# Feed-forward activations of both token halves turned in one go, the first input turned raw, and other orders at three places

## The chip, the cores and the metric

One core of a Trainium2 chip runs the whole program. The metric is the device time of one execution in microseconds (us); lower is better. Five engines work side by side, each through its own queue of instructions in a fixed order: PE (matrix products and transpositions), DVE (vector work), ACT (scalar activations and copies), POOL, and SP, which here does little but issue DMA transfers. An instruction waits at the head of its queue until what it needs is there, and all that stands behind it in that queue waits too.

## The reference, cut to what matters

The input is 256 tokens of 1024 features. Two layers follow, each a half feed-forward, a mixer, and another half feed-forward; the mixer is attention with pooling in layer 0 and a state-space layer (S5) with a gated output (GLU) in layer 1.

```
def _rmsnorm(x, g):
    xf = x.astype(jnp.float32)
    y = xf * lax.rsqrt(jnp.mean(xf * xf, axis=-1, keepdims=True) + EPS)
    return (y * g.astype(jnp.float32)).astype(x.dtype)

def _swiglu(h, w_gate, w_up, w_down):
    return (jax.nn.silu(h @ w_gate) * (h @ w_up)) @ w_down
...
    for layer in range(DEPTH):
        x = x + 0.5 * _swiglu(_rmsnorm(x, ffn_norm[layer, 0]), ffn_w_gate[layer, 0],
                              ffn_w_up[layer, 0], ffn_w_down[layer, 0])
        h = _rmsnorm(x, mix_norm[layer])
...
        x = x + mixed.astype(x.dtype)
        x = x + 0.5 * _swiglu(_rmsnorm(x, ffn_norm[layer, 1]), ffn_w_gate[layer, 1],
                              ffn_w_up[layer, 1], ffn_w_down[layer, 1])
```

The hidden width is 2816. So there are four feed-forwards, f = 0 to 3, with the attention mixer between f=0 and f=1 and the S5 mixer between f=2 and f=3.

## The kernel before, in words

**Products.** Each fp32 product is made of three matmuls on split operands (high times high, low times high, high times low). A weight arrives raw by DMA (tile `raw`, four buffers, issued on SP); ACT writes its high part `wh`, DVE the rest `wl`. Activations are split likewise: `hTh`/`hTl` is the normed input, transposed; `hh`/`hl` is the hidden activation, transposed. PE needs the contracted dimension on partitions, so both are transposed on PE (`tr`, a product with the identity, tile `sk` or `wk` in PSUM) before ACT and DVE split them.

**A feed-forward.** Tokens come in two tiles of 128, t = 0 and 1. The hidden width is done in 11 groups g of 256 columns. `GU(f, g, t, kh)` is the gate and up product of one tile for half kh of the 1024 features. Then ACT applies the activation (`sg`, L434), DVE makes the product (`pr`, L148), `hid_T` turns `pr` (two transpositions of 128x128) and has it split into `hh` and `hl`, and `dn(f, g, t)` is the down product, 12 matmuls of 512 columns into `acc`. `ffn_joint` runs the groups: 48 gate and up matmuls, `dn` of the group before for t=0, `hid_T` for t=0, `dn` for t=1, `hid_T` for t=1. `tail` ends a feed-forward: the last two `dn`s, the new x, the norm, and its transposition for what follows.

**Order.** Instructions are placed at build time by a scheduler. `prio(CHAIN)` lifts an instruction; `behind(names)` pins it behind instructions that `keep(name, ...)` has recorded; `hold` stops new weight splits until `release(names)`, which lets them go on behind the named instructions. S5 has a hand-written list of steps, `ORDER`: for each quarter k of the channels, `f` multiplies the input by the norm factor, `u` turns it, `w` is a product into the state space (32 small matmuls, copied out as `Sb` by ACT), `s` turns `Sb` back on PE and scans it on DVE, `d` and `o` are the direct and the output product, `h` makes the input of the GLU. An `x` with a number is so many warming matmuls, whose result nobody uses. `s5_put` copies the new x by 16 small DMAs on SP into the layout that S5 wants (tile `V`). While f=1 runs, `s5_build` prepares S5's matrices on DVE in its free time (tiles `E`, `X`, `b_q`, `b_st`).

**Start.** `first` loads the norm weights as one row, spreads it over all partitions by two products (`acc<-h,h`), multiplies x by it on DVE (`gained`), transposes the result and splits it; the squares for the norm factor are summed by ACT (`acc<-x`), and the factor `rstd` is applied later, in `sg` and `pr`.

Of the kernel before, what the change touches and what calls it, by code (L numbers as in the profile page):

```python
# [25 lines left out]
RING = 4  # L26
RAW = 4
CHAIN = 400
WARM = 20
WARM0 = 4  # L30
PACE = 0.8


# [8 lines left out]


ORDER = """
    f1 u1 hold s0 f2 u2 w1 s1 f3 u3 w2 s2 d0 o0 w3 s3 d1 d2 o1 x2 s4 h0 o2 d3 o3
"""
INV_FREQ = [
    1.0, 0.1939227432012558, 0.03760603070259094, 0.007292664609849453,
# [62 lines left out]
def trunk_kernel(ctx: ExitStack, tc: tile.TileContext, I, out):  # L111
# [16 lines left out]
    def sk(shape=(128, 512)):  # L128
        return work.tile(list(shape), F32, tag="sk", name="sk")
# [5 lines left out]
    def prio(n):  # L135
        return tc.high_priority(offset=n)

    def tt(o, a, b, op):
        return DVE.tensor_tensor(out=o, in0=a, in1=b, op=op)  # L139
# [19 lines left out]
    def tr(o, i, e):  # L159
        return PE.transpose(o, i, e)  # L160
# [8 lines left out]
    def keep(name, *ins):  # L169
        pins[name] = ins  # L170

    @contextmanager
    def behind(*names):

        with ExitStack() as st:
            for n in names:
                for i in pins.get(n, ()):
                    st.enter_context(tc.issue_after(i.ins))
            yield

    def hi_of(o, i):
        return ACT.activation(out=o, in_=i, func=AF.Copy)  # L182
# [77 lines left out]
    def emit_split(i):  # L260
        if units[i][0] == "K":
            n = units[i][1]
            tl = [wsp.tile([128, 2048], F32, tag=tg, name=f"K{n}") for tg in ("wh", "wl")]
            for q in range(2):
                c0 = 4096 * n + 2048 * q
                with behind("put"):
                    SP.dma_start(out=tl[q], in_=s5["dK"][:, c0:c0 + 2048])
            held[units[i]] = tl
            return
        if units[i][0] == "W":  # L270
            fill(2 * i)
            held[units[i]] = [raws.pop(2 * i + q).rearrange("p (a r j q n) -> p r j q a n", a=2, r=2, j=4, q=2)
                              for q in range(2)]
            return
        shape, places = pieces(units[i])
        h = wsp.tile([128, *shape], F32R, tag="wh", name="wh")
        l = wsp.tile([128, *shape], F32R, tag="wl", name="wl")
        for p in range(2):
            fill(2 * i + p)
            r = raws.pop(2 * i + p)  # L280
            s = places[p][1]
            with behind(*(["split"] if i + p else ["norm"])):
                for k in (slice(0, 2), slice(2, 4)) if i + p == 0 else (slice(None),):
                    hk, lk, rk = h[s][:, k], l[s][:, k], r[:, k]
                    keep("splits", hi_of(hk, rk), tt(lk, rk, hk.bitcast(F32), ALU.subtract))
                if i + p == 0:
                    pins["first"] = pins["splits"]
        held[units[i]] = (h, l)
# [26 lines left out]
    def acc_of(t):  # L315
        if t not in accs:
            accs[t] = [accp.tile([128, 512], F32, tag=f"acc{t}{c}", name=f"acc{t}{c}") for c in range(2)]
        return accs[t]
# [116 lines left out]
            stt(pr, ps[:, 1], rstds[f, t], sg, ALU.mult, ALU.mult)  # L435
        prods[f, g, t] = pr

    def hid_T(f, g, t):
        pr = prods.pop((f, g, t))
        o = slice(t * 128, (t + 1) * 128)  # L440
        if (f, g) not in hid:
            hid[f, g] = (hidp.tile([128, 2, 256], F32R, tag="hh", name="hh"),
                         hidp.tile([128, 2, 256], F32R, tag="hl", name="hl"))
        h, l = (x[:, :, o] for x in hid[f, g])
        ps = sk((128, 2, 128))
        with prio(CHAIN), behind("down" if g else "gu"):
            for m in range(2):
                tr(ps[:, m], pr[:, m * 128:(m + 1) * 128], ident)
            hi_of(h, ps)
            tt(l, ps, h.bitcast(F32), ALU.subtract)  # L450

    def down(f, g, t, c):
        w = held["d", f, g]
# [580 lines left out]
    def s5_put(t, c):  # L1034

        V = s5["V"]
        jobs = [(0, j) for j in (2 * c, 2 * c + 1)] + [(1, j) for j in range(4 * c)]
        for h, j in jobs:
            r = slice(64 * t + 16 * j, 64 * t + 16 * j + 16)
            c0 = 256 * j + 128 * h  # L1040
            with prio(CHAIN), behind("put", "rawW"):
                keep("put", SP.dma_start(out=V[r, h].rearrange("p t q g c -> p t (q g c)"), in_=xs[t][:, c0:c0 + 128]))

    def s5_scale(t, after):

# [182 lines left out]
    def glu(n, t, odd, terms, ks):  # L1228

        o = slice(t * 128, (t + 1) * 128)  # L1230
        if (n, t) not in glus:
            glus[n, t] = (sk if n % 2 else wk)((128, 2, 256))
        ps = glus[n, t]
        w = held["y", n, odd]
        for m in terms:
            x, y = (hTh, hTh, hTl)[m], w[m == 1]
            for k in ks:
                i = mm(ps, x[:, 2 * k + odd, o], y[:, k], odd == 0 and m == 0 and k == 0, odd == 1 and m == 2 and k == 3)
                if m == 2 and k == 1:
                    keep("glu", i)  # L1240
        if not (odd and terms[-1] == 2 and ks[-1] == 3):
            return
        th = tmp.tile([128, 256], F32, tag="t256", name="th")
        xv = xs[t][:, n * 256:(n + 1) * 256]
        with prio(CHAIN):
            ACT.activation(out=th, in_=ps[:, 1], func=AF.Tanh, scale=0.5)
            stt(th, th, 1.0, ps[:, 0], ALU.add, ALU.mult)
            stt(xv, th, 0.5, xv, ALU.mult, ALU.add)
        if n % 2:
            square(t, n // 2)  # L1250
# [6 lines left out]
    def S(fn, *uids):  # L1257
        steps.append((fn, uids))
# [22 lines left out]
    def dn(f, g, t, cs=(0, 1)):  # L1281
        for c in cs:
            if g < NG - 2:
                paced.add(len(steps))
            S(lambda c=c: down(f, g, t, c), ("d", f, g))

    def HID(f, g, t):
        S(lambda: hid_T(f, g, t))

    def ffn_joint(f, g0, g1):  # L1290

        for g in range(g0, g1):
            paced.add(len(steps))
            for kh in range(2):
                for t in range(2):
                    GU(f, g, t, kh)
                    if g == 1 and kh == 0:
                        HID(f, 0, t)
            if g < NG - 1:
                for t in range(2):  # L1300
                    dn(f, g - 1, t)
                    HID(f, g, t)

    def tail(f, fin_a, fin_b, each=lambda t, c: None):
        S(strict(f == 1))
        dn(f, NG - 2, 0, (0,))
        HID(f, NG - 1, 0)
        dn(f, NG - 2, 0, (1,))
        HID(f, NG - 1, 1)
        dn(f, NG - 1, 0, (0,))  # L1310
        S(lambda: x_update(0, 0.5, (0,)))
        each(0, 0)
        dn(f, NG - 1, 0, (1,))
        S(lambda: x_update(0, 0.5, (1,)))
        each(0, 1)
        fin_a()
        if f == 2:
            S(hold)
        dn(f, NG - 2, 1)
        if f == 1:  # L1320
            S(hold)
        dn(f, NG - 1, 1, (0,))
        S(lambda: x_update(1, 0.5, (0,)))
        each(1, 0)
        fin_b()
        dn(f, NG - 1, 1, (1,))
        S(lambda: x_update(1, 0.5, (1,)))
        each(1, 1)
# [27 lines left out]


    def first():
        row, one = hn[1][0:1], hn[0][0:1, 0:128]
        ACT.dma_start(out=row, in_=I["ffn_norm"][0, 0:1])  # L1360
        ACT.dma_start(out=ident, in_=cst[:, C_ID:C_ID + 128])
        for c in range(2):
            SP.dma_start(out=xs[0][:, c * 512:(c + 1) * 512], in_=I["x"][0, 0:128, c * 512:(c + 1) * 512])
        w = tmp.tile([128, 128], mybir.dt.bfloat16, tag="warm", name="warm")
        POOL.memset(w, 0.0)
        POOL.memset(one, 1.0)
        warm(WARM0, w)

        gvecs["f0"] = acc_of(1)
        for c in range(2):  # L1370
            mm(acc_of(1)[c], one, row[:, c * 512:(c + 1) * 512], True, True)
        fill(2 - RAW)
        for c in range(2):
            SP.dma_start(out=xs[1][:, c * 512:(c + 1) * 512], in_=I["x"][0, 128:256, c * 512:(c + 1) * 512])
        for c in range(2):
            square(0, c, acc_of(0)[c])
        gained(0, "f0")
        scaled(0, 0)
        warm(2, w)
        h_transpose(0)  # L1380
        pins["split"] = pins["hT"]
        ring.append(units[0])
        emit_split(0)
        state["split"] = 1
        with behind("first", "hT"):
            gained(1, "f0")

    def second():
        h_transpose(1, sk, "up")
        with behind("hT"):  # L1390
            for c in range(2):
                square(1, c, acc_of(0)[c])
        scaled(1, 0)
        accs.clear()
    S(first)

# [197 lines left out]
```

## Time and profile before

| what | value |
|---|---|
| median of three runs | 948.49 us (947.25 to 948.86) |
| the profiled execution | 948.75 us |
| its span in the trace | 947.0 us |
| PE busy | 927.9 us (98%) |
| DVE busy | 649.3 us (69%) |
| ACT busy | 445.9 us (47%) |
| mean granted clock of PE | 0.995 |

The time of an execution is some 1.75 us longer than the span of its trace. Busy shares are means over the whole span; in single stretches other engines decide. A granted clock of 1.00 is 2.4 GHz, 0.50 is 1.2 GHz.

### The profile page before, as it was taken

Reading aid. Unit: us, or ns where it says so; the run is one execution under the profiler, and the core shown is the slowest. Engines: PE = TensorE matmul, PEld = TensorE weight load, DVE = VectorE, ACT = ScalarE, POOL = GpSimd, SP = SyncE. Lnnn points to the kernel's source line nnn. Section 1 sums busy time; section 2 is a strip of 40 time slices with the busy share of each in tenths; the row PEclk is TensorE's granted clock in tenths of the full one; section 3 lists DMA queues with packets and bytes.
Section 4 is the critical chain, followed back from the end, with each engine's and each line's share of the span. In section 5 each row is a group of like instructions: output and inputs, shape, how many; then the busy total and the mean of one; then the engine's idle time right before and its main releaser. Section 6 shows DMA issues by size and latency. Waiting matters only on the chain.

```text
span 947.0 us, 13237 instructions
## 1 busy us (share of the span) xinstructions
PE 927.9 (98%) x5002; PEld 762.2 (80%) x5002; DVE 649.3 (69%) x1103; ACT 445.9 (47%) x653; POOL 60.2 (6%) x106
## 2 busy tenths in 40 slices
PE   9999999999999999999999999999879999999998
PEld 5888888889988888888788888888558788888886
DVE  5656754588867659999886557998487565554552
ACT  6544444455636444444454434445435464444440
POOL 0000000013020000000132001600000000000000
PEclk9999999999999999999999999999989999999999
DMA  7867666655476976566868655966855557556641
GB/s 242 274 194 210 197 185 197 192 159 159 134 202 200 200 201 204 156 190 183 281 200 288 186 178 160 259 184 213 292 187 177 179 174 225 178 183 198 195 136 44
DMA packets 149937, 184.59 MB, mean 195 GB/s; under 512 B 23153, under 2 KB 132657, under 8 KB 149106
## 3 DMA queue, kind: packets, MB, share of 16 engines
q1 hardware_dynamic: 146480, 175.29, 59.9%
q0 software_dynamic: 3248, 8.39, 3.5%
q8 instruction: 39, 0.64, 0.3%
q14 instruction: 24, 0.20, 0.1%
q10 hardware_dynamic: 146, 0.07, 0.0%
HBM read 173.24 MB, written 9.44 MB: 193 GB/s over the span
## 4 chain that ended last, share of the span: by engine, by line
PE 81%; DVE 12%; issue 2%; ACT 2%; DMA 1%; POOL 1%; SPq 0%; DVEq 0%; ACTq 0%; POOLq 0%
PE wk L101 47%; PE acc L101 26%; PE sk L101 7%; DVE wl L139 4%; DVE X L139 2%; DVE b_q L139 1%; POOL r L618 1%; DMA raw<-in_ffn_w_up_dram 1%; DVE b_t L139 1%; DVE hl L139 0%; DMA raw<-in_ffn_w_down_dram 0%; DVE qk L139 0%; ACT wh L182 0%; DVE pr L148 0%; ACT h L1082 0%
## 5 line engine op out<-in xcount | busy, mean ns | idle before, releaser
L139 DVE TENSOR_TENSOR wl<-raw,wh 128x1024 fp32r<-128x1024 f32 (+1 forms) x305 | 364.6, 1217 | 171.0 <-ACT wh L182 169.9
L182 ACT ACTIVATE wh<-raw 128x1024 fp32r<-128x1024 f32 (+1 forms) x305 | 312.7, 1052 | 254.6 <-PE wk L101 105.6
L101 PE MATMUL wk<-wh,hTh 128*128 128x512 f32 (+1 forms) x836 | 222.2, 385 | 1.2 <-DVE hTl L139 0.8
L101 PE MATMUL wk<-wl,hTh 128*128 128x512 f32 (+1 forms) x836 | 216.1, 377 | 0.1
L101 PE MATMUL wk<-wh,hTl 128*128 128x512 f32 (+1 forms) x836 | 215.1, 377 | 0.0
L101 PEld LDWEIGHTS wk<-wl,hTh 128*128 128x128 f32 x836 | 152.2, 189 | 30.0 <-DVE wl L139 0.5
L101 PEld LDWEIGHTS wk<-wh,hTl 128*128 128x128 f32 x836 | 151.8, 188 | 29.5
L101 PEld LDWEIGHTS wk<-wh,hTh 128*128 128x128 f32 x836 | 148.1, 189 | 28.2 <-DVE hTl L139 1.3
L101 PE MATMUL acc<-wh,hh 128*128 128x512 f32 x352 | 142.3, 404 | 1.3 <-ACT hh L182 1.3
L101 PE MATMUL acc<-wh,hl 128*128 128x512 f32 x352 | 138.8, 395 | 0.6 <-DVE hl L139 0.6
L101 PE MATMUL acc<-wl,hh 128*128 128x512 f32 x352 | 137.8, 392 | 0.0
L434 ACT ACTIVATE sg<-wk,rstd 128x256 f32<-128x256 f32 x88 | 41.6, 475 | 108.4 <-PE wk L101 103.9
L101 PEld LDWEIGHTS acc<-wh,hl 128*128 128x128 f32 x352 | 66.4, 189 | 16.3 <-DVE hl L139 1.7
L148 DVE SCALAR_TENSOR_TENSOR pr<-wk,rstd,sg 128x256 f32<-128x256 f32 x88 | 42.0, 479 | 53.0 <-ACT sg L434 52.9
L101 PEld LDWEIGHTS acc<-wh,hh 128*128 128x128 f32 x352 | 66.5, 189 | 14.1 <-ACT hh L182 1.5
L101 PEld LDWEIGHTS acc<-wl,hh 128*128 128x128 f32 x352 | 66.6, 189 | 12.8
L182 ACT ACTIVATE hh<-sk 128x256 fp32r<-128x256 f32 x88 | 32.7, 373 | 19.8 <-PE sk L101 19.7
L139 DVE TENSOR_TENSOR hl<-sk,hh 128x256 fp32r<-128x256 f32 x88 | 36.5, 418 | 3.7 <-ACT hh L182 3.7
L101 PE MATMUL sk<-ident,pr 128*128 128x128 f32 x176 | 33.6, 272 | 0.0
L101 PEld LDWEIGHTS sk<-ident,pr 128*128 128x128 f32 x176 | 24.1, 138 | 11.6 <-ACT b_br L930 0.3
L339 ACT ACTIVATE acc<-x 128x512 f32<-128x512 f32 x24 | 14.4, 600 | 25.9 <-DVE x L148 20.4
L139 DVE TENSOR_TENSOR hTl<-sk,hTh 128x512 fp32r<-128x512 f32 x24 | 17.4, 757 | 9.9 <-ACT hTh L182 9.9
(290 smaller groups left out, 627.0 us busy)
## 6 DMA issues: line engine op xcount, KB each, us to landing
raw<-in_ffn_w_up_dram SPq DMA_DIRECT2D x88, 512.0 KB
raw<-in_ffn_w_down_dram SPq DMA_DIRECT2D x88, 512.0 KB
raw<-in_ffn_w_gate_dram SPq DMA_DIRECT2D x87, 512.0 KB
raw<-in_ev_w_in_dram SPq DMA_DIRECT2D x16, 512.0 KB
raw<-in_s_w_glu_dram SPq DMA_DIRECT2D x16, 512.0 KB
raw<-in_ev_w_out_dram SPq DMA_DIRECT2D x8, 512.0 KB
K<-dK SPq DMA_DIRECT2D x4, 1024.0 KB
dK<-E POOLq DMA_DIRECT2D x36, 64.0 KB, 4.9
```

The lines of the kernel that those rows point to most:

```text
L101: i = f(*a, **k)
L139: return DVE.tensor_tensor(out=o, in0=a, in1=b, op=op)
L148: return DVE.scalar_tensor_tensor(out=o, in0=a, scalar=s, in1=b, op0=op0, op1=op1)
L182: return ACT.activation(out=o, in_=i, func=AF.Copy)
L339: keep("square", ACT.activation(out=into or acc_of(t)[c], in_=xs[t][:, s], func=AF.Square, scale=1.0 / 32.0, accum_out=sums[t][:, c:c + 1]))
L434: ACT.activation(out=sg, in_=ps[:, 0], func=AF.Silu, scale=rstds[f, t])
L618: POOL.tensor_tensor(out=r8, in0=s8, in1=mhalf.to_broadcast([128, 8]), op=ALU.pow)
```

## The change

There are five parts.

A. `hid_T` takes both token tiles: for groups 1 to 9 of each feed-forward the four transpositions stand in a row between the two `dn`s, ACT writes one `hh` of 128x512 and DVE one `hl` of 128x512, in place of two of 128x256 each. These are 36 places. The first and last groups keep the old form.

B. At the end of f=1, `hold` comes before the second half of the last group and `release("hid")` after the two `hid_T`, so the weight splits for f=2 go behind the `hh` and `hl`.

C. At the start the norm weights are loaded as 8x128 and turned by one transposition into a column form (`gT`); x is transposed as it is, and the split applies `gT` as a per-partition factor, one ACT copy and one DVE operation for each of 16 blocks of 128x128. The two spreading products, the four DVE products and two warming matmuls go; the four squares move behind the splits.

D. In S5 the puts have another order, so that the first half of every row group is issued by the ninth put on SP, and one put goes to ACT's queue; in `ORDER` the steps `w1 s1` and `w2 s2` stand ahead of `u2` and `u3`, with four and three warming matmuls beside them; 16 instead of 20 warming matmuls stand ahead of S5.

E. In the GLU the pin for the transposition of the next feed-forward's input (8 transpositions, `wk<-ident,h`) is moved from the last matmuls of the GLU to ten matmuls earlier.

```diff
-WARM = 20
-WARM0 = 4
+WARM = 16
+WARM0 = 5
...
-    f1 u1 hold s0 f2 u2 w1 s1 f3 u3 w2 s2 d0 o0 w3 s3 d1 d2 o1 x2 s4 h0 o2 d3 o3
+    f1 u1 hold s0 w1 s1 x4 f2 u2 w2 s2 x3 f3 u3 d0 o0 w3 s3 d1 d2 o1 x2 s4 h0 o2 d3 o3
...
-    def hid_T(f, g, t):
-        pr = prods.pop((f, g, t))
-        o = slice(t * 128, (t + 1) * 128)
+    def hid_T(f, g, *ts):
...
+        o = slice(ts[0] * 128, (ts[-1] + 1) * 128)
         h, l = (x[:, :, o] for x in hid[f, g])
-        ps = sk((128, 2, 128))
+        ps = sk((128, 2, len(ts) * 128))
         with prio(CHAIN), behind("down" if g else "gu"):
-            for m in range(2):
-                tr(ps[:, m], pr[:, m * 128:(m + 1) * 128], ident)
-            hi_of(h, ps)
-            tt(l, ps, h.bitcast(F32), ALU.subtract)
+            for n, t in enumerate(ts):
+                pr = prods.pop((f, g, t))
+                for m in range(2):
+                    tr(ps[:, m, n * 128:(n + 1) * 128], pr[:, m * 128:(m + 1) * 128], ident)
+            keep("hid", hi_of(h, ps), tt(l, ps, h.bitcast(F32), ALU.subtract))
...
-        jobs = [(0, j) for j in (2 * c, 2 * c + 1)] + [(1, j) for j in range(4 * c)]
-        for h, j in jobs:
+        if t == 0:
+            jobs = [(0, h, j) for h in range(c + 1) for j in range(2 * c * (1 - h), 2 * c * (1 - h) + 2)]
+        else:
+            jobs = [(1, 0, j) for j in (2 * c, 2 * c + 1)]
+            if c:
+                jobs += [(0, 1, 2), (0, 1, 3)] + [(1, 1, j) for j in range(4)]
+        for t, h, j in jobs:
...
-                if m == 2 and k == 1:
+                if odd == 0 and m == 2:
                     keep("glu", i)
...
+                if f == 1 and g == NG - 1 and kh:
+                    S(hold)
...
-                for t in range(2):
-                    dn(f, g - 1, t)
-                    HID(f, g, t)
+                dn(f, g - 1, 0)
+                HID(f, g, 0, 1)
+                dn(f, g - 1, 1)
...
         HID(f, NG - 1, 1)
+        if f == 1:
+            S(lambda: release("hid"))
...
+    def x_transpose(t, c, *after):
+
+        gT, o = gvecs["f0"], slice(t * 128, (t + 1) * 128)
+        ps = sk((128, 4, 128))
+        with prio(CHAIN), behind(*after):
+            for k in range(4):
+                tr(ps[:, k], xs[t][:, (4 * c + k) * 128:(4 * c + k + 1) * 128], ident)
+            for k in range(4):
+                h, l, g = hTh[:, 4 * c + k, o], hTl[:, 4 * c + k, o], gT[:, 4 * c + k:4 * c + k + 1]
+                keep("hT", ACT.activation(out=h, in_=ps[:, k], func=AF.Copy, scale=g),
+                     stt(l, ps[:, k], g, h.bitcast(F32), ALU.mult, ALU.subtract))
```

How the change moves instructions is seen at three places. The first is ACT at the end of f=1. `sg` belongs to the last group, `wh<-raw` 128x4x256 are weights of f=2, `hh` is the last group's hidden activation, `acc,ss<-x` are the squares of the new x. Before:

```order
L434 ACTIVATE sg<-wk,rstd 128x256 x2
L182 ACTIVATE wh<-raw 128x4x256 x2
L182 ACTIVATE hh<-sk 128x2x128 x2
L339 ACTIVATE acc_2858,ss<-x_81 128x512
L339 ACTIVATE acc_2859,ss<-x_81 128x512
L182 ACTIVATE wh<-raw 128x4x256 x2
L182 ACTIVATE hTh<-sk 128x4x128 x2
```

Now, at the same place:

```order
+L434 ACTIVATE sg<-wk,rstd 128x256 x2
+L182 ACTIVATE hh<-sk 128x2x128 x2
+L182 ACTIVATE wh<-raw 128x4x256 x2
+L339 ACTIVATE acc_2848,ss<-x_81 128x512
+L339 ACTIVATE acc_2849,ss<-x_81 128x512
+L182 ACTIVATE wh<-raw 128x4x256 x2
+L182 ACTIVATE hTh<-sk 128x4x128 x2
```

The two `hh` have moved ahead of two weight splits; DVE's `hl` have moved ahead of the `wl` of the same weights.

The second place is PE in the middle of S5, from the first product into the state space (`sk<-hTh,U`, step w0) on. `ident,h` are the steps u, `ident,Sb` the steps s. Before:

```order
L101 MATMUL sk<-hTh,U 32x2x64 x16
L101 MATMUL wk<-ident,h_85 128x128 x4
L101 MATMUL sk<-ident,Sb 128x128 x4
L101 MATMUL wk<-ident,h_86 128x128 x4
L101 MATMUL sk<-hTl,U 32x2x64 x16
L101 MATMUL sk<-ident,Sb 128x128 x4
L101 MATMUL wk<-ident,h_86 128x128 x4
L101 MATMUL sk<-rawW,U 32x2x64 x16
L101 MATMUL sk<-ident,Sb 128x128 x4
```

Now:

```order
L101 MATMUL sk<-hTh,U 32x2x64 x16
L101 MATMUL wk<-ident,h_85 128x128 x4
L101 MATMUL sk<-ident,Sb 128x128 x4
L101 MATMUL sk<-hTl,U 32x2x64 x16
L101 MATMUL sk<-ident,Sb 128x128 x4
L101 LDWEIGHTS warm
L101 MATMUL wk<-warm 128x512
```

Three more warming matmuls follow, then `ident,h_86`, the product with `rawW`, its `ident,Sb`, three warming matmuls, and the last `ident,h_86`. The steps w1 and s1 no longer stand behind u2, and w3's neighbour u3 stands behind s2.

The third place is ACT at the start, up to the first `sg`, from the last transposed blocks of the input on. Before:

```order
L182 ACTIVATE hTh<-sk 128x4x128 x2
L339 ACTIVATE acc_110,ss<-x_82 128x512
L348 ACT_TABLE_LOAD
L348 ACTIVATE pre<-x_82 128x1
L339 ACTIVATE acc_111,ss<-x_82 128x512
L182 ACTIVATE wh<-raw 128x4x256 x4
L434 ACTIVATE sg<-wk,rstd 128x256
```

Now:

```order
L182 ACTIVATE wh<-raw 128x4x256
L1406 ACTIVATE hTh<-sk,gT 128x128 x2
L339 ACTIVATE acc_201,ss<-x_81 128x512
L339 ACTIVATE acc_202,ss<-x_81 128x512
L339 ACTIVATE acc_201,ss<-x_82 128x512
L339 ACTIVATE acc_202,ss<-x_82 128x512
L348 ACT_TABLE_LOAD
L348 ACTIVATE pre<-x_82 128x1
L434 ACTIVATE sg<-wk,rstd 128x256 x2
```

All four squares and the second table load now stand directly ahead of the first two `sg`; six full weight splits stood ahead of the first `sg` before, now five. Ahead of ACT's first table load now stands the wait for `gT`, which DVE copies after PE has turned the row.

## Rows read from the trace of the kernel before

A timeline's row has the start on the device (us), the duration (us), engine, line, operation, out<-in, shape and count, and in brackets how long the engine stood idle before it and what ended that. A window's row has the stretch, its length, then busy time and (instructions) of PE, PE's weight loads, DVE, ACT and POOL, then PE's granted clock, the DMA engines' busy share and GB/s.

**Rows 1.** The page: busy time of PE, share of the span, instructions.
```profile
PE 927.9 (98%) x5002; PEld 762.2 (80%) x5002; DVE 649.3 (69%) x1103; ACT 445.9 (47%) x653; POOL 60.2 (6%) x106
```

**Rows 2.** Chain of waits in f=0 (start, duration, what); then PE's timeline after f=1.
```profile
103.28 2.72 PE acc L101 x12
106.00 0.22 PE sk L101 x2
106.22 2.77 PE acc L101 x12
...
477.19 1.03 PE L101 MATMUL sk<-ident,h 128*128 128x128 f32 x8
477.98 0.48 PE L101 MATMUL acc<-wh,hh 128*128 128x512 f32 x1
```

**Rows 3.** Timelines of DVE and PE: t=1's product, t=0's transpositions; last, window of f=1.
```profile
120.69 0.48 DVE L148 SCALAR_TENSOR_TENSOR pr<-wk,rstd,sg 128x256 f32<-128x256 f32 x1 [2.10 <-ACT sg L434]
122.71 0.38 PE L101 MATMUL sk<-ident,pr 128*128 128x128 f32 x2
433.26 0.48 DVE L148 SCALAR_TENSOR_TENSOR pr<-wk,rstd,sg 128x256 f32<-128x256 f32 x1
432.23 0.38 PE L101 MATMUL sk<-ident,pr 128*128 128x128 f32 x2
345.00:470.00 125.00, 123.10 (x554) 100.38 (x553) 117.75 (x290) 56.63 (x75) 4.28 (x8) 1.00 0.64 193
```

**Rows 4.** Timelines of PE and ACT at the end of f=1; last, window with clock.
```profile
463.24 0.39 PE L101 MATMUL acc<-wh,hh 128*128 128x512 f32 x1
467.90 0.50 PE L101 MATMUL acc<-wh,hh 128*128 128x512 f32 x1 [1.31 <-ACT hh L182]
469.22 0.79 PE L101 MATMUL acc<-wh,hl 128*128 128x512 f32 x1 [0.59 <-DVE hl L139]
466.52 1.06 ACT L182 ACTIVATE wh<-raw 128x1024 fp32r<-128x1024 f32 x1 [1.66 <-DMA raw<-in_ffn_w_up_dram]
467.48 0.64 ACT L182 ACTIVATE hh<-sk 128x256 fp32r<-128x256 f32 x2
470.00:472.00 2.00, 2.00 (x7) 1.51 (x6) 1.17 (x4) 0.00 (x0) 0.00 (x0) 0.50 1.08 406
```

**Rows 5.** Timelines of SP, DVE and ACT in S5; last, window with clock.
```profile
667.53 12.53 SPq L1042 DMA_DIRECT2D V<-x  x16
679.54 0.76 DVE L139 TENSOR_TENSOR h<-V,rV 128x256 f32<-128x256 f32 x2 [3.44 <-DMA V<-x]
688.62 0.69 DVE L139 TENSOR_TENSOR h<-sk,E 128x512 f32<-128x512 f32 x1 [0.79 <-PE sk L101]
700.13 0.69 DVE L139 TENSOR_TENSOR h<-sk,E 128x512 f32<-128x512 f32 x1 [1.04 <-PE sk L101]
683.43 2.02 ACT L1082 ACTIVATE h<-V,rV 128x64 f32<-128x64 f32 x8
693.00:695.00 2.00, 2.00 (x28) 1.57 (x31) 1.92 (x4) 0.00 (x0) 0.00 (x0) 0.50 0.85 265
```

**Rows 6.** Timeline of PE at the end of the GLU.
```profile
756.40 0.74 PE L101 MATMUL wk<-wh,hTh 128*128 128x512 f32 x2 [0.84 <-DVE hTl L139]
```

**Rows 7.** Timelines of ACT and PE at the start; last, window with ACT's busy time.
```profile
3.60 0.60 ACT L339 ACTIVATE acc<-x 128x512 f32<-128x512 f32 x1 [0.63 <-DMA x<-in_x_dram]
...
15.19 1.28 ACT L348 ACT_TABLE_LOAD   x1
16.48 0.20 ACT L348 ACTIVATE pre<-x 128x1 f32<-128x1 f32 x1
21.77 0.47 ACT L434 ACTIVATE sg<-wk,rstd 128x256 f32<-128x256 f32 x1 [0.22 <-PE wk L101]
24.23 1.07 PE L101 MATMUL wk<-wh,hTh 128*128 128x512 f32 x4
0.00:24.00 24.00, 21.69 (x86) 14.42 (x86) 13.75 (x20) 16.02 (x25) 2.03 (x14) 1.00 0.77 243
```

More of the change, by code (lines that the diff above doesn't have):

```diff
@@ L281, in emit_split @@
             s = places[p][1]
-            with behind(*(["split"] if i + p else ["norm"])):
+            with behind("split"):
                 for k in (slice(0, 2), slice(2, 4)) if i + p == 0 else (slice(None),):
@@ L1036, in s5_put @@
         V = s5["V"]
-        jobs = [(0, j) for j in (2 * c, 2 * c + 1)] + [(1, j) for j in range(4 * c)]
-        for h, j in jobs:
+        if t == 0:
[5 more added lines that the diff above has]
+        for t, h, j in jobs:
             r = slice(64 * t + 16 * j, 64 * t + 16 * j + 16)
             c0 = 256 * j + 128 * h
+            own = (t, h, j) == (1, 0, 3)
             with prio(CHAIN), behind("put", "rawW"):
-                keep("put", SP.dma_start(out=V[r, h].rearrange("p t q g c -> p t (q g c)"), in_=xs[t][:, c0:c0 + 128]))
+                i = (ACT if own else SP).dma_start(out=V[r, h].rearrange("p t q g c -> p t (q g c)"), in_=xs[t][:, c0:c0 + 128])
+                if not own:
+                    keep("put", i)
     def s5_scale(t, after):
@@ L1285, in dn, with HID @@
             S(lambda c=c: down(f, g, t, c), ("d", f, g))
-    def HID(f, g, t):
-        S(lambda: hid_T(f, g, t))
+    def HID(f, g, *ts):
+        S(lambda: hid_T(f, g, *ts))
     def ffn_joint(f, g0, g1):
@@ L1358, in first @@
     def first():
-        row, one = hn[1][0:1], hn[0][0:1, 0:128]
-        ACT.dma_start(out=row, in_=I["ffn_norm"][0, 0:1])
+        row = hn[1][0:8, 0:128]
+        ACT.dma_start(out=row, in_=I["ffn_norm"][0, 0].rearrange("(k p) -> k p", p=128))
         ACT.dma_start(out=ident, in_=cst[:, C_ID:C_ID + 128])
@@ L1365, in first @@
         POOL.memset(w, 0.0)
-        POOL.memset(one, 1.0)
         warm(WARM0, w)
-        gvecs["f0"] = acc_of(1)
-        for c in range(2):
-            mm(acc_of(1)[c], one, row[:, c * 512:(c + 1) * 512], True, True)
+        gT = gvecs["f0"] = per.tile([128, 8], F32, name="gT")
+        with prio(CHAIN):
+            ps = sk((128, 8))
+            tr(ps, row, ident[0:8, 0:8])
+            DVE.tensor_copy(out=gT, in_=ps)
         fill(2 - RAW)
@@ L1374, in first @@
             SP.dma_start(out=xs[1][:, c * 512:(c + 1) * 512], in_=I["x"][0, 128:256, c * 512:(c + 1) * 512])
[L1375 to L1380, printed above, removed]
+        x_transpose(0, 0)
         pins["split"] = pins["hT"]
@@ L1384, in first @@
         state["split"] = 1
-        with behind("first", "hT"):
-            gained(1, "f0")
+        hold()
+    def x_transpose(t, c, *after):
[8 more added lines that the diff above has]
+                     stt(l, ps[:, k], g, h.bitcast(F32), ALU.mult, ALU.subtract))
     def second():
-        h_transpose(1, sk, "up")
+        x_transpose(1, 0, "up")
+        release()
+        x_transpose(0, 1, "up")
+        x_transpose(1, 1, "up")
         with behind("hT"):
-            for c in range(2):
-                square(1, c, acc_of(0)[c])
-        scaled(1, 0)
+            for t in range(2):
+                for c in range(2):
+                    square(t, c, acc_of(0)[c])
+                scaled(t, 0)
         accs.clear()
```

## The prediction

> **What bounds the kernel now.** I read the page first: PE is busy 98% of the span [rows 1], so time can be won in three ways only: less work on PE, gaps of PE closed, or stretches at the lower clock avoided. Then I read the chain of waits for the ordinary group, then the timelines of PE, DVE, ACT and SP at the places that the diff touches, and the windows there for the clock. What the reader is to see: in an ordinary group PE goes from one down product to the next through a pair of transpositions without waiting [rows 2], and the four other places (start, end of f=1, S5, end of the GLU) are the ones with gaps [rows 4 to 7]. The sum is made against the profiled execution, 948.75 us; the median of the three runs is 948.49, 0.26 less, so a result within a microsecond of mine is not told apart from mine. About 0.2% (1.9 us) is what a measurement of this kernel can tell from no change.
>
> **A, the merged transpositions.** A pair of transpositions stands 0.22 us in the chain, and the twelve matmuls behind it take 2.77 us where twelve with no transposition ahead take 2.72 [rows 2]. Eight in a row need 477.98 - 477.19 = 0.79 us until the next product starts [rows 2], 0.1 each. So four cost 4 x 0.1 to 4 x 0.11 = 0.4 to 0.44 us and two pairs 0.44; what the merge saves is one of two disturbed starts, 0.05, and a hundredth: 0.06 us at each of 36 places, 2.1 us in all. ACT and DVE save an instruction's fixed part as well, but neither is waited for in these stretches.
>
> The price: the transposition of t=1 now stands where that of t=0 stood, one down product (2.7 us) earlier, and PE waits there for the later `pr`. In an ordinary group there is room: `pr` of t=1 ends at 120.69 + 0.48 = 121.17, and the transpositions of t=0 start at 122.71, 1.5 us later [rows 3]. In f=1 there is not always: DVE is busy 117.75 of 125 us with S5's matrices, and in the group at 432 `pr` of t=1 ends at 433.74 while PE reaches the place at 432.23, 1.5 us too late [rows 3]. What is late then is everything on PE behind it, the second down product and the next group. The group shown is the worst that I found of those in f=1, and DVE has somewhat less to do after the merge. Bounds: no wait anywhere (0), or 1.5 us in three groups (4.5). I take one such wait, 1.5. A together: 2.1 - 1.5 = 0.6 gained; between 2.1 gained and 2.4 lost.
>
> **B, the end of f=1.** ACT's weight split at 466.52 waited 1.66 us for its DMA, and the two `hh` stood behind it in ACT's queue and came at 467.48; PE, which needs them, stood 1.31 us, then 0.59 more for `hl`, and after that the granted clock was 0.50 (the 1.2 GHz level) in the window from 470 to 472 [rows 4]. The change puts `hh` ahead of those splits, so it comes right behind its transposition. What it is worth: from 463.24 to the transpositions of the next input at 477.19 [rows 2, 4] PE has 42 matmuls and two pairs of transpositions. At 2.72 / 12 = 0.227 us each that is 9.5 us, with 0.54 for the two pairs 10.06, so PE would be there at 473.3: 3.9 us won, of which 1.9 are the two waits and 2.0 the lower clock. Not all may come: the displaced weight splits now stand on DVE between the updates of x and the norm that these transpositions need, so DVE may be late by some tenths. I take 3.5; bounds 2.0 (DVE eats what the clock gives back) and 3.9.
>
> **C, the start.** PE's share is lighter, since the two spreading products are gone, but what decides is when `sg` and `pr` of the first group are done, because the next group's products need their PSUM tile; in the old order PE went through without waiting for it, at 24.23 [rows 7]. All of ACT's work now stands in one row ahead of `sg`. Its sum: ACT was busy 16.02 us of the first 24, of which 0.47 are that `sg` [rows 7], leaving 15.55. One full weight split less (1.06, the duration of the one at 466.52 [rows 4]); four turned copies of 128x512 become 16 of 128x128 with a factor: eight copies of 128x64 with a factor take 2.02 us [rows 5], 0.25 each, so 16 take 4.0 to 4.8; an ACT pass over 128x512 took 0.60 [rows 7], so four took 2.4. Net 15.55 - 1.06 + 1.6 to 2.4 = 16.1 to 16.9. ACT can't begin before `gT`, which needs PE's transposition and a DVE copy behind the first data; the first half of x was there at 3.60 [rows 7], so I put it at 4.0. Without any further wait `sg` starts at 20.1 to 20.9, against 21.77 before: up to 1.6 won. With waits of PE and DMA between, as before (the old order had several), up to 24 and more: some 2 lost, since `pr` (0.48 [rows 3]) has to follow before PE can go on. The old order left PE, whose product stream reached 24.23, 24.23 - (21.77 + 0.47 + 0.48) = 1.5 us of cover over this path at most; a lateness of `sg` within that is hidden unless PE's own stream has come earlier. I take 0 for C; bounds 2.0 gained and 1.5 lost.
>
> ACT's next instruction began at 16.48, right where the table load from 15.19 with 1.28 us ended [rows 7]. The Trainium skill (ScalarE: Activation LUTs, What ACT_TABLE_LOAD costs) adds a drain of about 1.38 us to each load; by that the path to `sg` would be 1.38 us longer for the load that now stands directly ahead of it, and C would lose about as much. The trace does not show this drain here, so the sum goes by the row.
>
> **D, S5.** The first product of V waited 3.44 us for the puts and started at 679.54; the 16 puts take 12.53 us of SP's queue [rows 5], 0.78 each with the waits for x in it. It needed the first twelve of them; now the ninth is enough. Three puts at 0.63 to 0.78 are 1.9 to 2.3; I take 1.9, since some of the waits stay. The put that goes to ACT stands behind the last square and nothing waits behind it for long. From here to the GLU DVE's scans are the chain. It stood 0.79 at 688.62 and 1.04 us at 700.13 for PE's turned-back `Sb` [rows 5]; PE was late because step w stood behind a u that waited for ACT's eight small copies (2.02 us [rows 5]), and the second time also because the clock was 0.50 around 694 [rows 5]. With w1 s1 and w2 s2 ahead of those, both waits can go: 1.83. ACT's copies for u2 and u3 come later, and their cover is a scan step of DVE, longer than 2.02. Together 1.9 + 1.8 = 3.7; bounds 1.0 (only part of the puts' gain, the clock falls as before) and 4.2.
>
> **E, the GLU.** PE stood 0.84 us for `hTl` at 756.40 [rows 6]. The transpositions come ten matmuls earlier, 10 x 0.227 = 2.3 us, more than the wait; they need the new x of the first tile, which is ready some time before. 0.85 gained; bounds 0.5 and 1.0.
>
> **Sum.** 0.6 + 3.5 + 0 + 3.7 + 0.85 = 8.65 us; 948.75 - 8.65 = 940.1 us.
>
> **Rivals.**
> 1. The forecast, each term near its value: 938.5 to 941.7, chance 0.40.
> 2. S5 and f=1 give only part. For it: PE's gaps in S5 stay long, and after such a gap the clock was 0.50 around 694 [rows 5]; warming matmuls fill some of it only. Against it: the new order closes two of the gaps. D gives only the puts' 1.9, B only 2.0: 940.1 + 1.8 + 1.5 = 943.4. From 941.7 to 946.5: chance 0.26.
> 3. The start gains. For it: PE has two spreading products and DVE four multiplications less ahead of the first split blocks. Against it: ACT's row above. If `sg` starts at 20.5 and DVE is not late in f=1 either: 940.1 - 1.6 - 1.5 = 937.0. Below 938.5: chance 0.15.
> 4. The start loses: ACT waits between its blocks and all squares come late; 1.5 us by the bound above, 941.6, and with drained table loads 943. Chance 0.07.
> 5. Slower than before: PE waits for `pr` of t=1 in all of f=1. Place: each of nine merged transpositions there. Price: the lateness of the group shown, 1.5 us [rows 3], nine times 13.5 instead of the 1.5 taken, and 952.1 us. It decides from 8.65 + 1.5 + 1.9 = 12 us of waits, 1.3 in each group. Against it: DVE gets no more work than before, and a PE that waits gives DVE time to catch up. Chance 0.05.
> 6. No change that can be told (946.6 to 950.4), if the waits only move on to the next one: chance 0.07.
>
> **How the numbers follow.** The predicted time is case 1's, 940.1. The range has 8 in 10 if it takes in the bounds of case 2 and most of case 3: 936.0 to 946.5. Faster by over 0.2%: cases 1 to 4, 0.88; within: 0.07; slower: 0.05.
>
> **What would show it.** Right: no idle time of PE behind the two `hh` at the end of f=1 and a clock of 1.00 there; the first `h<-V,rV` of S5 about 2 us sooner behind f=2's end; no wait for PE in the two `h<-sk,E`; no wait for `hTl` at the end of the GLU; four transpositions in a row followed by a down product with no wait on `pr`, except in f=1. Wrong: PE idle on `pr` in several groups; PE idle at about 24 us on `pr` or `sg`; a clock of 0.50 at the start of the next stage after S5's new order.

## The result: 1.4% slower, where 0.9% faster was forecast

| | before | changed |
|---|---|---|
| median | 947.87 us (4 runs, 946.85 to 948.86) | 961.78 us (4 runs, 958.76 to 963.12) |
| profiled execution, span | 948.75, 947.0 | 963.12, 961.3 |
| ratio | | 1.0142 (95%: 1.0115 to 1.017) |

The page of the changed kernel answers to [rows 1]: PE has one instruction less and is busy 9.2 us longer, at the same mean clock (0.995).

```profile
PE 937.1 (97%) x5001; PEld 763.9 (79%) x5001; DVE 649.6 (68%) x1076; ACT 445.5 (46%) x629; POOL 60.1 (6%) x105
```

That is the first hint: not only gaps were added, the products themselves take longer. The chain of waits in an ordinary group of f=0 (start, duration, what) shows which; it answers to [rows 2].

```profile
113.73 0.44 PE sk L101 x4
114.16 2.75 PE acc L101 x12
116.91 11.19 PE wk L101 x48
128.10 2.72 PE acc L101 x12
```

The four transpositions are there, 0.44 us, and the down products take 2.75 and 2.72 as expected. But the 48 gate and up products (`wk`) take 11.19 us. In the kernel before, the same view shows:

```profile
92.35 10.93 PE wk L101 x48
```

There a pair of transpositions stands directly ahead, which disturbs the first of them; without it they would take 48 x 0.2267 = 10.88. So each product takes 0.0065 us more, and no engine is waited for. In these products PE holds a block of `hTh` or `hTl` and streams `wh` or `wl` through it. All of the 44 groups have it, and so have the products of the mixers that stream 512 columns, 2388 in all (2196 written to `wk`, 96 each to `sk` and `acc`): as an estimate 2388 x 0.0065 = 15.5 us. The 408 products with these operands that stream 256 columns don't have it: from one start to the next it is 0.120 us before and 0.117 now (medians over the trace). The down products, which stream the same tiles `wh` and `wl` and hold `hh` or `hl`, don't have it either.

The second loss is at the start. ACT's timeline of the changed kernel, up to the first `sg` [rows 7]:

```profile
5.55 1.28 ACT L1406 ACT_TABLE_LOAD   x1 [5.55 <-DVE gT L1386]
6.84 0.37 ACT L1406 ACTIVATE hTh<-sk,gT 128x128 fp32r<-128x128 f32 x1
7.63 0.37 ACT L1406 ACTIVATE hTh<-sk,gT 128x128 fp32r<-128x128 f32 x1 [0.42 <-DVE hTl L148]
8.41 0.37 ACT L1406 ACTIVATE hTh<-sk,gT 128x128 fp32r<-128x128 f32 x1 [0.42 <-DVE hTl L148]
...
15.54 0.63 ACT L1406 ACTIVATE hTh<-sk,gT 128x128 fp32r<-128x128 f32 x2 [4.00 <-PE sk L101]
16.33 0.63 ACT L1406 ACTIVATE hTh<-sk,gT 128x128 fp32r<-128x128 f32 x2 [0.16 <-DVE hTl L148]
...
26.72 1.28 ACT L348 ACT_TABLE_LOAD   x1
28.02 0.20 ACT L348 ACTIVATE pre<-x 128x1 f32<-128x1 f32 x1
28.13 0.82 ACT L434 ACTIVATE sg<-wk,rstd 128x256 f32<-128x256 f32 x2
```

Each of the first four blocks takes 0.79 us, since ACT's copy waits for DVE's operation on the block before; the next eight take 0.79 for every two. In between ACT stands 4 us for PE; `sg` starts at 28.13, 6.4 us later than before. PE's timeline shows what that does:

```profile
5.02 0.24 PE L101 MATMUL sk<-ident,h 8*128 8x8 f32 x1 [1.71 <-DMA ident<-in_cst_dram]
10.14 1.32 PE L101 MATMUL wk<-wh,hTh 128*128 128x256 f32 x4 [3.83 <-ACT wh L182]
29.16 1.81 PE L101 MATMUL wk<-wh,hTh 128*128 128x512 f32 x4 [2.17 <-DVE pr L148]
...
42.44 0.39 PE L101 MATMUL acc<-wh,hh 128*128 128x512 f32 x1
```

PE waits 2.17 us for `pr` at 29.16, and the granted clock falls: the window from 30 to 32 has 0.50, the 1.2 GHz level.

```profile
30.00:32.00 2.00, 2.00 (x6) 1.58 (x5) 2.00 (x2) 2.00 (x3) 0.00 (x0) 0.50 0.05 10
```

The first down product starts at 42.44 us; before it was 35.65:

```profile
35.65 0.39 PE L101 MATMUL acc<-wh,hh 128*128 128x512 f32 x1
```

6.8 us are lost there, some 0.3 of them to the longer products. They come in three steps: PE's own stream of products is through at 26.99 where it was at 24.23, 2.8 us late; then come the 2.17 us of waiting; and the twelve products from 29.16 to 33.59, most of them at the lower clock, take 4.43 us, where 12 x 0.2267 = 2.72, so 1.7 more.

The end of f=1 is as forecast. From its first down product at 475.17 to the transpositions there is no wait and the clock stays at 1.00; 10.03 us, where 463.24 to 477.19 was 13.95 [rows 2, 4]:

```profile
475.17 0.39 PE L101 MATMUL acc<-wh,hh 128*128 128x512 f32 x1
...
485.20 1.03 PE L101 MATMUL sk<-ident,h 128*128 128x128 f32 x8
```

In S5 the puts brought nothing. SP's queue and DVE, answering to [rows 5]:

```profile
678.19 14.23 SPq L1050 DMA_DIRECT2D V<-x  x15
690.48 0.76 DVE L139 TENSOR_TENSOR h<-V,rV 128x256 f32<-128x256 f32 x2 [3.73 <-DMA V<-x]
```

Fifteen puts take longer on SP than sixteen did. From the first small product that makes the norm factor (`sk<-by,sel`, 672.86 before, 683.51 now) to the first `h<-V,rV` it is 6.97 us, before 6.68. The two later waits of DVE for `Sb` are gone, but two stretches of PE got longer. The first product into the state space (`sk<-hTh,U`) takes 1.94 us, behind a gap of 2.24 us and at a granted clock of 0.50 in the window from 692 to 694; before it was 1.08:

```profile
681.20 1.08 PE L101 MATMUL sk<-hTh,U 128*32 128x128 f32 x32 [0.30 <-DVE U L1103]
```

Now, with a stop of PE near the end of S5 and the first product of the GLU:

```profile
692.14 1.94 PE L101 MATMUL sk<-hTh,U 128*32 128x128 f32 x32 [0.27 <-DVE U L1113]
...
715.79 1.87 PE L101 MATMUL sk<-ident,V 128*128 128x128 f32 x8 [2.23 <-issue]
...
721.68 0.73 PE L101 MATMUL wk<-wh,hTh 128*128 128x512 f32 x2
```

From the first `sk<-by,sel` to the first product of the GLU it is 38.17 us, before 37.09. At the end of the GLU the wait for `hTl` [rows 6] is gone: no such row is left among PE's waits.

Lateness of the changed kernel against the kernel before, at five points of PE's timelines: 6.8 us at the first down product, 8.0 at the transposition of f=2's input, 10.7 at the first `sk<-by,sel`, 11.7 at the first product of the GLU, 14.3 at the end.

### The profile page after: what moved, and what is told of

It reads as the page before. It is cut to its first block, busy times and chain, and to the rows that moved or that the text cites. A ratio compares the mean times of both kernels' runs of the same rounds, so it can differ in the third digit from the quotient of the medians.

```text
span 961.3 us, 13195 instructions
## 1 busy us (share of the span) xinstructions
PE 937.1 (97%) x5001; PEld 763.9 (79%) x5001; DVE 649.6 (68%) x1076; ACT 445.5 (46%) x629; POOL 60.1 (6%) x105
## 4 chain that ended last, share of the span: by engine, by line
PE 91%; DVE 3%; ACT 2%; issue 1%; DMA 1%; POOL 1%; ACTq 0%; DVEq 0%; SPq 0%; POOLq 0%
PE wk L101 55%; PE acc L101 28%; PE sk L101 8%; DVE wl L139 1%; POOL r L619 1%; DMA V<-x 1%; DVE qk L139 0%; ACT h L1092 0%; DMA ident<-in_cst_dram 0%; ACT hTh L1406 0%; DVE hTl L148 0%; DVE sc L139 0%; DVE s L617 0%; DVE mx L659 0%; POOL rstd L376 0%
## 5 line engine op out<-in xcount | busy, mean ns | idle before, releaser
L182 ACT ACTIVATE wh<-raw 128x1024 fp32r<-128x1024 f32 (+1 forms) x305 | 308.0, 1051 | 238.5 <-PE wk L101 124.5
L101 PE MATMUL wk<-wl,hTh 128*128 128x512 f32 (+1 forms) x836 | 221.2, 383 | 0.0
L101 PE MATMUL wk<-wh,hTl 128*128 128x512 f32 (+1 forms) x836 | 219.3, 381 | 0.0
L101 PEld LDWEIGHTS wk<-wh,hTh 128*128 128x128 f32 x836 | 151.4, 189 | 40.9 <-ACT wh L182 4.2
L182 ACT ACTIVATE hh<-sk 128x512 fp32r<-128x512 f32 (+1 forms) x52 | 27.6, 531 | 33.8 <-PE sk L101 33.8
L139 DVE TENSOR_TENSOR hl<-sk,hh 128x512 fp32r<-128x512 f32 (+1 forms) x52 | 31.3, 606 | 6.1 <-ACT hh L182 6.0
L101 PE MATMUL sk<-ident,pr 128*128 128x128 f32 x176 | 27.7, 272 | 0.0
L101 PEld LDWEIGHTS sk<-ident,pr 128*128 128x128 f32 x176 | 22.1, 139 | 7.1 <-ACT b_br L931 0.3
L339 ACT ACTIVATE acc<-x 128x512 f32<-128x512 f32 x24 | 14.4, 599 | 20.9 <-DVE x L148 16.4
L976 POOL DMA_DIRECT2D dK<-E x36 | 18.8, 545 | 84.3 <-ACT E L957 74.2
```

Of the source, the lines that this page charges most:

```text
L101: i = f(*a, **k)
L339: keep("square", ACT.activation(out=into or acc_of(t)[c], in_=xs[t][:, s], func=AF.Square, scale=1.0 / 32.0, accum_out=sums[t][:, c:c + 1]))
L976: POOL.dma_start(out=dK[16 * tp:16 * tp + 16, :, tau], in_=Kf[16 * (7 - lag):16 * (7 - lag) + 16])
```

## The experiments

The kernel before was run beside each series, on another chip, where its median was 949.5 to 951.6 us and single runs differed more. Traces are compared where runs differ by little. The changed kernel minus before was 1.0142 in ratio; each ratio below is against the kernel before of its own series.

### Why the products take longer

The tile `gT` that the new start needs is allocated in the persistent pool: 32 bytes a partition, at address 49824 behind `h1`. Every tile allocated later lies 32 bytes further up (`wh` at 66240 in place of 66208), while `hTh` (25248) and `hTl` (33440) stay. Eight kernels test that this is the cause.

```diff
-        gT = gvecs["f0"] = per.tile([128, 8], F32, name="gT")
+        gT = gvecs["f0"] = per.tile([128, 16], F32, name="gT")[:, 0:8]
```

> The changed kernel with one thing altered: the new tile gT of the norm weights takes 64 bytes a partition instead of 32, so that all tiles allocated behind it (raw, wh, wl, hh, hl and so on) lie 64 instead of 32 bytes further up than in the kernel before, while hTh and hTl stay where they were. Theory 1 (place in memory): 48 gate and up products take 11.19 us in the changed kernel and 10.93 before because wh and wl have moved by 32 bytes against hTh and hTl; with 64 they take 10.9 again, and with some 2500 such products at 0.0066 us each the time falls by about 15 us, to 946 to 948, the start still about 6 us late. Rival (the merged hh and hl, or the other order of ACT and DVE, disturb the products): 11.19 us stay and the time is 962.

952.47 us (ratio 1.0024, 1.0000 to 1.0048), 9.3 less than the changed kernel by this edit alone. The theory was right in kind, not in amount:

```profile
130.97 10.99 PE wk L101 x48
```

The next two add the 32 bytes to the kernel before, at two places:

```diff
         POOL.memset(one, 1.0)
+        pad = per.tile([128, 8], F32, name="pad")
+        POOL.memset(pad, 0.0)
```

> The kernel before with an unused tile of 32 bytes a partition (written once by POOL at the start) allocated where the changed kernel has gT; nothing else. Theory 1 (place in memory): 48 gate and up products take 11.2 us instead of 10.93, and the time rises by 14 to 17 us, to 962 to 965. Rival (the merged hh and hl, or the order): 10.93 stay and the time is 948.

962.04 us (1.0124, 1.0073 to 1.0174). An unused tile, with nothing else of the change, gives nearly the whole loss:

```profile
126.14 11.20 PE wk L101 x48
```

The other place is ahead of all of them:

```diff
     DVE.memset(mhalf, -0.5)
+    pad = per.tile([128, 8], F32, name="pad")
+    POOL.memset(pad, 0.0)
```

> The kernel before with the same unused 32 bytes allocated ahead of x and hTh, so that hTh, hTl, wh, wl, hh and hl all move by 32 bytes together. If what counts is where wh and wl lie against hTh and hTl, the products stay at 10.93 us per 48 and the time at 948. If it is the absolute place of wh and wl, which is the same here as in the changed kernel, they take 11.2 us and the time is 962 to 965.

951.09 us (1.0006, 0.9981 to 1.0030), no difference, and the products are back, with `wh` and `wl` at the very addresses of the run before it:

```profile
126.99 10.93 PE wk L101 x48
```

So it is not the address of the streamed tiles, but where they lie against `hTh` and `hTl`. Then the changed kernel with nothing moved:

```diff
-        gT = gvecs["f0"] = per.tile([128, 8], F32, name="gT")
+        gT = gvecs["f0"] = hn[0][:, 0:8]
```

> The changed kernel with gT kept in the first eight columns of h0, a tile that is free at that time, so that no other tile moves against the kernel before. Theory 1 (place in memory): 48 gate and up products take 10.88 to 10.93 us, and the time is that of the kernel before plus about 6.5 for the start and 1 for S5, less 2 for the merges, 4 for the end of f=1 and 1 for the GLU: 949 (948 to 951). Rival (64 bytes in the last series left 10.99 us because the merged hh and hl disturb the products a little): 10.99 stay and the time is 952 to 955.

946.99 us (0.9965, 0.9942 to 0.9988), a microsecond under the range expected. The products are at what was worked out for a run with no transposition ahead:

```profile
132.10 10.88 PE wk L101 x48
```

All else of the change is in this kernel, so the rival (the merged `hh` and `hl` disturb the products) is out. Between its median and that of the changed kernel lie 14.8 us, between the spans of the two profiled executions 13.4 (947.9 and 961.3).

How the cost goes with the distance was tried on the kernel before, with 64, 96 and 128 bytes at the place of `gT`:

> The kernel before with an unused tile of 64 bytes (written once) where 32 bytes cost 0.27 us per 48 products. Theory (the place of wh and wl against hTh and hTl alone sets it): 48 gate and up products behind a pair of transpositions take 10.99 + 0.05 = 11.04 us, as the changed kernel with a 64-byte gT showed 10.99 without transpositions ahead, and the time rises by about 5 to 954. Rival (the 10.99 came from the merged hh and hl): 10.93 and no change of time.

952.80 us (1.0039, 1.0007 to 1.0070), 11.01 us for 48 products.

> The same with 96 bytes. If what counts is whether the distance between the two operands is a multiple of 64 bytes, 48 products take 11.2 us and the time is 962; if the cost grows or falls with the distance in another way, something else between 10.93 and 11.2.

963.55 us (1.0133, 1.0104 to 1.0161; two runs), 11.21.

> The same with 128 bytes. If the distance counts modulo 128 bytes, 48 products take 10.93 us and the time is that of the kernel before, 948; if it counts modulo more, some of the loss stays, as with 64 bytes.

959.06 us (1.0085, 1.0053 to 1.0118; two runs), 11.17. The chains of waits of these three, in the same order:

```profile
127.48 11.01 PE wk L101 x48
```
```profile
128.53 11.21 PE wk L101 x48
```
```profile
128.24 11.17 PE wk L101 x48
```

32 and 96 bytes cost about 0.27 us in 48 products, 64 cost 0.08, 128 cost 0.24. The guess that 128 bytes would be free fell; the cost is no simple function of the distance modulo 64 or 128 bytes, and the rule stays open. The last one moves `hTl` along and leaves `hTh`:

```diff
     hTh = per.tile([128, 8, SEQ], F32R, name="hTh")
+    pad = per.tile([128, 8], F32, name="pad")
+    POOL.memset(pad, 0.0)
```

> The kernel before with the unused 32 bytes allocated between hTh and hTl: hTh stays, and hTl, wh and wl move by 32 bytes together. Theory (what counts is the distance from the held operand hTh or hTl to the streamed wh or wl): in one and the same execution the four-matmul runs with hTh start 0.933 us apart and those with hTl 0.907, as before; 48 products take 11.1 us and the time rises by two thirds of what 32 bytes behind both cost, to 957 to 959. Rival (the absolute place of wh and wl, or any of the three distances, slows all products alike): 0.933 for all runs and 962, or 0.907 for all and 948.

957.64 us (1.0071, 1.0046 to 1.0095). 48 products take 11.09, where two thirds of 11.20 and one third of 10.93 are 11.11:

```profile
125.78 11.09 PE wk L101 x48
```

The rival wanted 10.93 or 11.20. In this one execution the products also separate, if less cleanly than expected: from one start to the next it is 0.234 us where `hTh` is held and `wh` streamed, 0.232 with `hTh` and `wl`, and 0.227 with `hTl` and `wh`, whose distance is as before (medians over the trace).

### What the start costs

The next keeps the start of the kernel before and all else of the change:

> The changed kernel with the start of the kernel before (norm weights spread by two products, x multiplied ahead of its transposition, four warming matmuls, no gT, nothing moved in memory); the merges, the end of f=1, S5 and the GLU as changed. Theory (the start costs 6 to 7 us): 6.5 less than with gT in h0, some 942 to 943, and the first down product starts at about 35.7 us. Rival (the start's loss is hidden later, by DMA or by weight splits that are late anyway): less than 3 us between the two.

943.07 us (0.9918, 0.9886 to 0.9949). Its profile ends 6.7 us earlier than that of the kernel with `gT` in `h0` (spans 941.2 and 947.9), as expected; the medians differ by 3.9 only, since the runs of the latter spread over 945.4 to 949.8 and the profiled one was near the top. So the new start costs 4 to 7 us, and the rival (less than 3) is out.

Then the new start, with `gT` in `h0`, and ACT's copies and DVE's operations no longer in turns:

```diff
-            for k in range(4):
-                h, l, g = hTh[:, 4 * c + k, o], hTl[:, 4 * c + k, o], gT[:, 4 * c + k:4 * c + k + 1]
-                keep("hT", ACT.activation(out=h, in_=ps[:, k], func=AF.Copy, scale=g),
-                     stt(l, ps[:, k], g, h.bitcast(F32), ALU.mult, ALU.subtract))
+            ps = [(ps[:, k], hTh[:, 4 * c + k, o], hTl[:, 4 * c + k, o], gT[:, 4 * c + k:4 * c + k + 1]) for k in range(4)]
+            i = [ACT.activation(out=h, in_=p, func=AF.Copy, scale=g) for p, h, l, g in ps]
+            j = [stt(l, p, g, h.bitcast(F32), ALU.mult, ALU.subtract) for p, h, l, g in ps]
+            for n in range(4):
+                keep("hT", i[n], j[n])
```

> The changed kernel with gT in h0, where for each four blocks of the input the four copies of ACT are written in the program ahead of the four operations of DVE, instead of in turns. Theory (in turns, each copy of ACT waits for DVE's operation on the block before, 0.79 us a block instead of 0.25): the first four copies take 1.2 us instead of 2.7, the first sg starts 2 to 4 us sooner than with gT in h0 alone, and the time is 2 to 4 us less than that one's. Rival (the first product waits for the weights, and sg for the squares that stand behind everything): less than 1 us.

944.23 us (0.9935, 0.9911 to 0.9960), 2.8 less than in turns. ACT's timeline:

```profile
6.77 1.14 ACT L1405 ACTIVATE hTh<-sk,h 128x128 fp32r<-128x128 f32 x4
...
24.82 0.46 ACT L434 ACTIVATE sg<-wk,rstd 128x256 f32<-128x256 f32 x1
```

Four blocks take 1.14 us, and `sg` starts 3.1 us sooner than with `gT` in `h0` in turns (27.94). The first down product starts at 37.63 in place of 42.10, still 2 later than before: PE waits 0.71 us for `pr`, which stands behind the squares and the table load.

### S5

The put on ACT's queue goes back to SP, with the old start:

```diff
-            own = (t, h, j) == (1, 0, 3)
+            own = False
```

> As the one with the old start, but the put that went to ACT's queue stays on SP, in its place of the order. Theory (the put on ACT's queue holds back a later put on SP, which must wait for the same completion semaphore): the stall of the first h<-V,rV begins earlier to end, this instruction starts 1.5 to 2 us sooner after the last matmul of f=2, and the time falls by 1.5 to 2. Rival (the puts are bound by their landing, not by their issue): within 0.7 us of the other.

941.48 us (0.9918, 0.9886 to 0.9950), 1.6 less than with that put on ACT; the runs overlap (940.8 to 944.9 against 940.5 to 943.7), so the trace has to say it. From the first `sk<-by,sel` (668.40 and 667.41) to the first `h<-V,rV` (675.68 and 673.78) it is 7.28 us with the put on ACT and 6.37 without: 0.9 won, half of what the theory asked, and only 0.3 less than in the kernel before. With the put on ACT, issued at 669.25, the ninth on SP goes out at 673.02, 1.6 us behind the eighth (671.45); the program has it wait for the completion semaphore that ACT's put had taken in the rotation:

```profile
671.45 0.60 SPq L1050 DMA_DIRECT2D V<-x  x1
673.02 0.55 SPq L1050 DMA_DIRECT2D V<-x  x1
```

That part of the theory is right. What is left is the eighth put. In the program it takes over the completion semaphore of the last load of S5's weights (`rawW`), and it goes out when that load has landed: landing at 674.36 and put at 674.38 in the kernel before, 669.92 and 669.94 here. Counted from the first `sk<-by,sel` that is 1.5 us before and 2.5 here, so 1.0 of the 1.3 us that two puts fewer behind it win is lost. From the last put that it needs (676.90 before, 671.20 here) to DVE's start it is 2.6 us in both.

Last, the old order of the steps with its 20 warming matmuls, with the new order of the puts, all on SP, and the old start:

```diff
-WARM = 16
+WARM = 20
...
-    f1 u1 hold s0 w1 s1 x4 f2 u2 w2 s2 x3 f3 u3 d0 o0 w3 s3 d1 d2 o1 x2 s4 h0 o2 d3 o3
+    f1 u1 hold s0 f2 u2 w1 s1 f3 u3 w2 s2 d0 o0 w3 s3 d1 d2 o1 x2 s4 h0 o2 d3 o3
```

> As the one with the old start and all puts on SP, but with S5's steps in the order of the kernel before and its 20 warming matmuls; the new order of the puts stays. Theory (the new order of steps shortens DVE's chain by about 1.2 us and keeps the clock up, and PE's pause without a visible cause behind the second quarter's output takes most of it back): the chain of DVE from the first h<-V,rV to the last G gets 1.2 us longer again, but the time changes by less than 1. Rival (the new steps bring 1.8 as forecast): 1.5 to 2 us more.

943.25 us (0.9925, 0.9901 to 0.9950; runs 941.3 to 945.0): not to be told from the new order by the times, whose medians are 1.8 apart with overlapping runs, so the rival is judged by the traces. From the first `sk<-by,sel` to the first product of the GLU it is 36.1 us, with the new steps 36.5, before 37.1. DVE's chain, from the first `h<-V,rV` to the end of the last `G<-rot,rot`, is 675.13 to 701.95 = 26.8 us, and 673.78 to 698.80 = 25.0 with the new steps. So the new order does win the 1.8 us on DVE that were forecast, more than this expectation's 1.2, and they don't reach the GLU. Between the end of DVE's chain and the first product of the GLU it is 2.4 us with the old steps and 5.1 with the new. PE takes them back, in the run with the new steps:

```profile
694.30 1.14 PE L101 MATMUL acc<-X,G 64*32 64x128 f32 x62
698.42 0.40 PE L101 MATMUL acc<-X,G 64*32 64x128 f32 x2 [2.98 <-issue]
```

PE stops 2.98 us in the middle of a row of small products and waits for nothing that the profile shows.

## Why the prediction was wrong, point by point

**The step that failed** is one that the prediction didn't have. It took each product that the change leaves alone at its duration before (0.227 us), and so had no term for what a new tile does to the addresses of the others. That term is 12 to 15 us by the runs with and without the 32 bytes (962.04 against 949.54 in the kernel before, 961.78 against 946.99 in the changed one). The rest of the change, with nothing moved, is a little faster than the kernel before (ratio 0.9965).

**C, the start**, was taken at 0 with a loss of 1.5 as the bound; it costs 4 to 7. The work in ACT's row was forecast well: from ACT's first instruction to `sg` it is 22.6 us, of which 6.3 are waits, so 16.2 of work, where 16.1 to 16.9 were forecast. Two other steps failed. ACT's first instruction comes at 5.55, not at 4.0, since the transposition for `gT` waits for `ident` (1.71 us, PE's row at 5.02). And the waits between, whose cost was put at some 2 us and then taken at 0, are 4.00 us for PE's transpositions and 2.3 us in turns with DVE; 5.55 + 16.2 alone would have put `sg` at 21.8, where it stood before. The run with the turns undone won 2.8 us back. The cover of 1.5 us was not there either, since PE's own stream came 2.8 us later. The sign that the prediction named for this, PE idle on `pr`, is the wait at 29.16. The rival "the start loses" had the right mechanism (ACT waits between its blocks, the squares come late) and priced it at 1.5 us, where 4 to 7 were lost.

The Trainium skill (ScalarE: Activation LUTs, What ACT_TABLE_LOAD costs) adds about 1.38 us of drain to a table load. The trace does not show it here either: the next instruction starts at 28.02, where the load from 26.72 with 1.28 us ends.

**A, the merged transpositions**, was right: 10.88 + 2.72 + 0.44 + 2.75 = 16.79 us a group with `gT` in `h0`, against 16.86 before, so 0.07 where 0.06 were forecast. The wait of 1.5 us for `pr` in f=1 didn't come: among PE's waits in the changed kernel the only one for `pr` is that at the start. The slower rival (PE waits for `pr` in all of f=1) had the right sign for the wrong reason.

**B** was forecast at 3.5 and is 3.9 by the two traces. The weight splits that it puts on DVE between the updates of x make nothing late.

**E** was forecast at 0.85; the wait of 0.84 is gone.

**D, S5**, was forecast at 3.7 and brings nothing (37.16 us against 37.09 from `sk<-by,sel` to the GLU, with `gT` in `h0`; 38.17 in the changed kernel). The puts' 1.9 were counted on SP's queue alone: the one sent to ACT's queue holds back a later one, and with that undone 0.3 is left against before, since the eighth put waits for the weights of S5 to land. The steps' 1.8 are won on DVE and lost on PE's stop.

So the sum, per part and by the traces: A 36 x 0.07 = -2.5, B -3.9, D 0, E -0.8, C +6.7, the place in memory +13.4 (the spans with `gT` in `h0` and with it in a tile of its own): +12.9, where 14.4 was measured between the profiled executions.

The version with the old start and all puts on SP keeps A, B, E and the new S5: 941.48 us, ratio 0.9918 (0.9886 to 0.9950), ahead of both kernels.

## What to carry to other kernels

Where a kernel is bound by PE, compare the spacing of untouched products in the two profiles first: 0.0065 us on some 2400 products outweighed everything else that was edited here. A new small tile in a pool that others are allocated behind is a change to all of them; put it into a tile that is free at the time, or repeat the measurement with an unused tile of the same size. And where two engines work through the blocks of one tile in turns, write one engine's part ahead of the other's: in turns four copies took 2.7 us, apart 1.14.

## What the runs showed of the hardware that was not expected

The time of a product of 128x512 depends on how far its streamed tile lies from its held tile. With no transposition ahead, 48 of them take 10.88 us at the first distance, 11.19 with 32 bytes more and 10.99 with 64: 0.2267, 0.2331 and 0.2290 us each. Behind a pair of transpositions, 48 take 10.93 at first, and 11.20, 11.01, 11.21 and 11.17 with 32, 64, 96 and 128 bytes more. If both tiles move together by 32 bytes they take 10.93 again. Why the distance counts, and by which rule, was not settled.

PE's stop in S5 without a visible cause goes with a packet of the instruction queue. The windows of 0.2 us that hold it, by the view of DMA queues (queue, kind: packets, MB, share of 16 engines), and PE's next start in the timeline: kernel before 702.4, next start 704.82; changed kernel 713.2, 715.79; old start 698.2, 700.64; old start with all puts on SP 696.0, 698.42. The packet of the last of these:

```profile
q8 instruction: 1, 0.02, 32.0%
```

In all four PE goes on 2.4 to 2.6 us after the start of that window. Four more runs (`gT` in `h0`, pieces apart, 32 bytes in the kernel before, old steps of S5) have such stops of 0.7 to 2.6 us in this stretch, and each ends 2.4 to 2.5 us after the start of such a packet; other packets of this queue pass without a stop. It looks as if PE, which runs through over a hundred small instructions in 1.1 us there, were out of fetched instructions; no run changed that alone, so it is argued, not shown.
